# Nine instead of seven weight tiles ahead of two layer norms, with the first pair copied out of PSUM

## The chip, the core and the metric

The kernel runs on one core of a Trainium2 chip. The metric is device time per execution in microseconds (us). Before the change it is 1212.32 us, the median of three runs (1210.94 to 1214.39). The profile is of one execution of its own, which took 1212.16 us; its instructions span 1210.3 us of that, so 1.9 us lie around the span.

## The reference, cut to what matters

The reference computes two transformer blocks over 256 tokens of width 1024, in fp32. Block 2 has two layers. Each ends in a gated feed-forward network (FFN) that is fed by a layer norm:

```python
for l in range(DEPTH_2):                       # 2 layers
    y = even_mixer(...) if l % 2 == 0 else odd_mixer(...)
    x = layer_norm(alpha * x + y, ln_g[l, 0], ln_b[l, 0])       # the norm of this case
    y = conv_ffn(x, ffn_w_up[l], ffn_conv_w[l], ffn_conv_b[l], ffn_w_down[l])
    x = layer_norm(alpha * x + y, ln_g[l, 1], ln_b[l, 1])

def layer_norm(x, g, b):
    return (x - mu) * rsqrt(var + eps) * g + b
def conv_ffn(x, w_up, conv_w, conv_b, w_down):
    a, g = split(x @ w_up, 2)                  # w_up: 1024 x 5632
    return (gelu(causal_dwconv3(g) + conv_b) * a) @ w_down
```

The change touches the place where the layer norm `ln_g[l, 0]` runs into `x @ w_up`, in both layers.

## The kernel before

**Layout.** Activations lie feature by feature: 8 slices of 128 features on the partitions, 256 tokens along the row. `w_up` comes in 44 tiles of 1024 x 128 (512 KB each). One tile gives 128 output features, a *slice* here. Two slices (a and g of the same features) make a pair, and the gate needs both.

**Split arithmetic.** TensorE multiplies a rounded fp32 type, so each operand x is split into a high part h and a low part l = x - h. `wload` (L313) does it for weights: SP issues the DMA into `raw`, ScalarE casts `raw` to `hi` (L321), VectorE subtracts to `lo` (L322). A slice then takes 24 matmuls: 8 feature slices k, and for each hi times h (L329), hi times l (L330), lo times h (L331).

**The bridge.** A layer norm needs sums over all features of its input z, then a reciprocal square root on GpSimd, then a pass over z. TensorE would stand still meanwhile. So `layer_norm` (L1058) does two things side by side. It makes the normalized activations `nh`, `nl` in the usual way (L1076, L1077, and the split in L516 and L517). And through `raw_scaled` (L527) it makes `xh`, `xl` = z times g at once, with g and b as two more columns, so that the first weight tiles can be multiplied by these *raw* activations without waiting for the norm. Such a raw slice has 258 columns; when the row of means and deviations (`lnrow`, L1067) is there, `fix` (L1086) turns it into the right one: VectorE copies the two extra columns to `wgb` (L1090), ScalarE makes the shift from them (L1091), VectorE multiplies the slice in PSUM by the deviation row (L1093, out `sq`) and adds the shift (L1094, out `fx`). `NRAW` = 7 slices go this way: three pairs and the first slice of the fourth. From slice 8 on, `gemm_pairs` (L349) uses `nh` and `nl`.

**Banks.** PSUM has eight banks: four belong to the tag `a`, three to `g`, one to `m`. The raw slices take a whole bank each: the four `a`, then the three `g` (`places`, L1080). After them slice 8, whose partner is raw slice 7, takes the next `a` bank, and the later pairs go round four `a` and three `g` banks (`ring`, L623), a pair per bank. A bank can be written again when its last reader is done. For a raw slice that is VectorE's L1093.

**Order.** The order on each engine is worked out before the run by a scheduler that estimates times; each engine then runs its own list in that order, and waits at semaphores. `tc.high_priority` moves weight loads and the norm forward in it. The five buffers of `hi` and of `lo` are used in turn.

The bridge of layer 0 comes at 660 to 704 us of the span (bridge 1 here), that of layer 1 at 1005 to 1044 us (bridge 2). The norm in front of the odd mixer uses the same `layer_norm` with the tag `csb0` and its own number of raw slices.

Of the kernel before, what the change touches and what calls it, by code (L numbers as in the profile page):

```python
# [20 lines left out]
P = 128  # L21
S = 256
# [7 lines left out]
LAM_INIT = 0.8 - 0.6 * math.exp(-0.3 * 0)  # L30
MAGIC = 12582912.0
WPRI = 300
NRAW = 7
NRMS = 12
ORDER = ("kv0 ks w0 q w1 c0 tm c1 ckv kr CS0 CS1 CO0 kn CS2 CO1 CS3 CO2 kd CO3 cq uk uv uq DS0 DS1 DO0 DS2 DO1 DS3 "
         "DO2 DO3").split()
# [221 lines left out]
def _program(ctx, tc, nc, a, offs, dump):  # L258
    V, ACT, G, PE = nc.vector, nc.scalar, nc.gpsimd, nc.tensor
# [11 lines left out]
    pg = pool(ctx, "pg", 3, space=PSUM)  # L271
    pa = pool(ctx, "pa", 4, space=PSUM)
# [3 lines left out]
    def T(pl, shape, tag, dt=F32, **k):  # L276
        cnt[0] += 1
        return pl.tile(list(shape), dt, tag=tag, name="%s_%d" % (tag, cnt[0]), **k)
# [217 lines left out]
    def row_bcast(cols, at=None):  # L496
        rb = T(*(at or (pm,)), [P, len(cols) * P], "g" if at else "m")
        for j, c in enumerate(cols):
            mm(rb[:, j * P:(j + 1) * P], bc(c, [P, P]), ident, start=True, stop=True)
        return rb  # L500
# [13 lines left out]
    def split(src, h, l, scale=None):  # L514
        if scale is None:
            ACT.copy(h, src)  # L516
            tt(l, src, h, op=sub)  # L517
        else:
            act(h, src, AF.Copy, scale=scale)
            stt(l, src, scale, h, op0=mult, op1=sub)  # L520
# [6 lines left out]
    def raw_scaled(x, g, b, n):  # L527
        uh, ul = T(hp, [P, 8, n], "xh", F32R), T(hp, [P, 8, n], "xl", F32R)
        with tc.high_priority(LPRI):
            for c, v in zip(range(S, n), (g, b)):  # L530
                split(v, uh[:, :, c], ul[:, :, c])
            for k in range(8):
                act(uh[:, k, 0:S], x[:, k, :], AF.Copy, scale=g[:, k:k + 1])
                stt(ul[:, k, 0:S], x[:, k, :], g[:, k:k + 1], uh[:, k, 0:S], op0=mult, op1=sub)
        return dict(h=uh, l=ul, n=n)
# [505 lines left out]
    def ln_stats(z):  # L1041
        with tc.high_priority(LPRI):
            st = T(pm, [P, 4], "m")
            col_sums(st, [folded(*tiles(z, 8)), folded(*squares(z, 8))])
        return st

    def ln_rstd(st):
        nmu, mq = T(sm, [P, 2], "lnmu"), T(sm, [P, 2], "lnmq")
        act(nmu, st[:, 0:2], AF.Copy, scale=-1.0 / D)
        act(mq, st[:, 2:4], AF.Copy, scale=1.0 / D, bias=1e-5)  # L1050
        var = T(sm, [P, 2], "lnv")
        G.tensor_tensor(var, nmu, nmu, op=mult)
        G.tensor_tensor(var, mq, var, op=sub)
        r = T(sm, [P, 2], "lnr")
        G.tensor_tensor(r, var, mhalf[:, :2], op=ALU.pow)
        return nmu, r

    def layer_norm(z, g, b, h, l, xn, pl, tr_="lnrow", tf="fx"):  # L1058
        st = ln_stats(z)
        raw = raw_scaled(z, g, b, S + 2)  # L1060
        with tc.high_priority(LPRI):
            nmu, r = ln_rstd(st)
            nr = T(sm, [P, 2], "lnn")
            G.tensor_tensor(nr, nmu, r, op=mult)
            rb = row_bcast([r[:, 0:1], r[:, 1:2], nr[:, 0:1], nr[:, 1:2]])
            rs = T(pl, [P, 2, S], tr_)
            ACT.copy(rs.rearrange("p a s -> p (a s)"), rb)  # L1067
            rr, rn = rs[:, 0], rs[:, 1]
            for k, w in ((0, 1), (1, 1), (2, 2), (4, 2), (6, 2)):
                s2 = slice(k, k + w)  # L1070
                f = T(tp, [P, w, S], "sqa", bufs=2)
                u = T(tp, [P, w, S], "sq", bufs=3)
                for n in range(w):
                    c = k + n
                    act(f[:, n, :], rn, AF.Identity, scale=g[:, c:c + 1], bias=b[:, c:c + 1])  # L1075
                    stt(u[:, n, :], z[:, c, :], g[:, c:c + 1], rr, op0=mult, op1=mult)  # L1076
                tt(xn[:, s2, :], u, f, op=add)  # L1077
                split(xn[:, s2, :], h[:, s2, :], l[:, s2, :])

        places = iter([(pa, "a")] * 4 + [(pg, "g")] * 3)  # L1080

        def banks(n):
            raw["tiles"] -= n
            return [T(pl_, [P, raw["n"]], tag) for pl_, tag in (next(places) for _ in range(n))]

        def fix(rps):  # L1086
            f = T(pl, [P, 2, S], tf, bufs=2)
            for n in range(len(rps)):
                wgb = T(sm, [P, 2], "wgb")
                V.tensor_copy(wgb, rps[n][:, S:S + 2])  # L1090
                act(f[:, n, :], rn, AF.Identity, scale=wgb[:, 0:1], bias=wgb[:, 1:2])  # L1091
                t = T(tp, [P, S], "sq", bufs=3)
                tt(t, rps[n][:, 0:S], rr, op=mult)  # L1093
                tt(f[:, n, :], f[:, n, :], t, op=add)  # L1094
            return f

        raw.update(fix=fix, banks=banks, tiles=NRAW if tf == "fx" else NROD)
        return raw

# [709 lines left out]
    for i in range(2):  # L1809
        def norm(j, zt, xn):  # L1810
            g, b = C["ln_g%d%d" % (i, j)], C["ln_b%d%d" % (i, j)]
            return lambda h, l, pl, *tags: layer_norm(zt, g, b, h, l, xn, pl, *tags)

        if i == 1:
            with ExitStack() as ph:
                ap_ = pool(ph, "od", 1)
                cod = T(ap_, [P, a["cod"].shape[1]], "cod")
                nc.scalar.dma_start(cod, a["cod"])
                KO = {k: cod[:, o:o + n] for k, (o, n) in off_o.items()}
                W = T(ap_, [P, 8, S], "W")  # L1820
                nc.scalar.dma_start(W, hankel(0, 8))
                h, l = T(ap_, [P, 8, S], "oh", F32R), T(ap_, [P, 8, S], "ol", F32R)
                raw = norm_od(h, l, ap_, "ockv", "csb0")
                yh, yl = odd(ap_, h, l, W, KO, raw)
                z = T(xp, [P, 8, S], "x")
                gemm_pairs("od_out", range(4), 8, yh, yl, join=True, **residual_a(xa, z))
        dump("z%d0" % i, z)
        xa, z0 = T(xp, [P, 8, S], "x"), z
        z = T(xp, [P, 8, S], "x")
        ffn(norm(0, z0, xa), "g_up%d" % i, "g_dn%d" % i, C["gcw%d" % i], C["gcb%d" % i], False,  # L1830
            residual_a(xa, z))
        dump("z%d1" % i, z)
        if i == 0:
            xa = T(xp, [P, 8, S], "x")
            norm_od = norm(1, z, xa)
# [13 lines left out]
```

## Time and profile before

| | |
|---|---|
| median of three runs | 1212.32 us |
| profiled execution, and its span | 1212.16 us, 1210.3 us |
| TensorE busy | 1169.8 us, 97% |
| VectorE busy | 888.8 us, 73% |
| ScalarE busy | 691.8 us, 57% |
| GpSimd busy | 59.8 us, 5% |
| mean granted TensorE clock | 0.988 of full speed |

Busy time is the time in which an engine has an instruction in work. [...] The rows below give starts in us from the start of the span. [...]

### The profile page before, as it was taken

What the parts mean: (1) busy time and instruction counts of PE and PEld (TensorE: products, weight loads), DVE (VectorE), ACT (ScalarE), POOL (GpSimd) and SP (SyncE); (2) the same over time, 40 slices, a digit from 0 to 9 for tenths busy, and PEclk for the clock granted to TensorE, in tenths of its full rate; (3) what the DMA queues carried; (4) which work ended last, traced back from release to release, by engine and by line L of the source; (5) the groups of instructions that cost most, each with busy time, mean ns of one, the idle gap of its engine ahead of it and who ended that gap; (6) DMA issues with size and microseconds to landing.
All of it is one profiled execution on the core that took longest, in us unless ns stands there. A gap on an engine that the chain in (4) does not pass through costs nothing.

```text
span 1210.3 us, 23541 instructions
## 1 busy us (share of the span) xinstructions
PE 1169.8 (97%) x9370; PEld 1111.2 (92%) x9370; DVE 888.8 (73%) x1704; ACT 691.8 (57%) x1229; POOL 59.8 (5%) x61
## 2 busy tenths in 40 slices
PE   7889999999999999999999899999999999999997
PEld 7889989999999999899988899998988789999986
DVE  8969856866688887667565886667696768976654
ACT  5684544655566765446355675544675666755541
POOL 4000000100000000000001000001000001000010
PEclk9899999999999999999999999999998999999998
DMA  7424435664356556656423566656862125665560
GB/s 269 154 87 128 152 123 181 210 192 149 108 172 199 185 177 182 194 175 219 164 89 112 158 189 178 184 177 192 296 206 95 56 74 189 206 186 181 161 204 35
DMA packets 61276, 199.41 MB, mean 165 GB/s; under 512 B 8502, under 2 KB 12398, under 8 KB 60910
## 3 DMA queue, kind: packets, MB, share of 16 engines
q1 hardware_dynamic: 54864, 191.60, 49.7%
q10 hardware_dynamic: 6302, 6.32, 1.6%
q8 instruction: 73, 1.20, 0.4%
q14 instruction: 37, 0.30, 0.1%
HBM read 196.28 MB, written 1.60 MB: 163 GB/s over the span
## 4 chain that ended last, share of the span: by engine, by line
PE 85%; DVE 6%; ACT 3%; DMA 3%; issue 2%; POOL 1%; SPq 0%; DVEq 0%; ACTq 0%
PE g L330 11%; PE g L331 11%; PE g L329 11%; PE a L329 7%; PE a L330 7%; PE a L331 7%; PE a L394 5%; PE g L394 4%; PE a L396 3%; DVE lo L322 2%; PE g L340 2%; PE g L338 2%; PE g L339 2%; PE g L396 2%; DMA W<-vec 2%
## 5 line engine op out<-in xcount | busy, mean ns | idle before, releaser
L322 DVE TENSOR_TENSOR lo<-raw,hi 128x1024 fp32r<-128x1024 f32 (+3 forms) x359 | 427.9, 1196 | 185.8 <-ACT hi L321 178.1
L321 ACT CAST hi<-raw 128x1024 fp32r<-128x1024 f32 (+3 forms) x359 | 363.5, 1020 | 349.4 <-PE g L330 129.1
L329 PE MATMUL g<-xh,hi 128*128 128x256 f32 (+1 forms) x616 | 175.9, 286 | 8.1 <-ACT xh L569 7.9
L330 PE MATMUL g<-xl,hi 128*128 128x256 f32 (+1 forms) x624 | 179.4, 288 | 0.2
L331 PE MATMUL g<-xh,lo 128*128 128x256 f32 (+1 forms) x616 | 175.5, 285 | 1.3 <-DVE lo L322 1.2
L329 PE MATMUL a<-nh,hi 128*128 128x256 f32 x560 | 159.6, 286 | 4.6 <-ACT sqa L1075 2.8
L330 PE MATMUL a<-nl,hi 128*128 128x256 f32 x560 | 159.2, 285 | 0.9 <-DVE nl L517 0.9
L331 PE MATMUL a<-nh,lo 128*128 128x256 f32 x560 | 159.0, 284 | 0.0
L329 PEld LDWEIGHTS g<-xh,hi 128*128 128x128 f32 x616 | 117.4, 191 | 9.6 <-ACT xh L569 8.1
L330 PEld LDWEIGHTS g<-xl,hi 128*128 128x128 f32 x624 | 119.3, 191 | 1.5 <-DVE xl L570 0.7
L331 PEld LDWEIGHTS g<-xh,lo 128*128 128x128 f32 x616 | 117.0, 190 | 2.3 <-DVE lo L322 1.9
L329 PEld LDWEIGHTS a<-nh,hi 128*128 128x128 f32 x560 | 108.2, 194 | 5.7 <-ACT sqa L1075 2.9
L330 PEld LDWEIGHTS a<-nl,hi 128*128 128x128 f32 x560 | 108.3, 193 | 1.1 <-DVE nl L517 1.1
L331 PEld LDWEIGHTS a<-nh,lo 128*128 128x128 f32 x560 | 108.3, 193 | 0.0
L394 PE MATMUL a<-mx,hi 128*128 128x512 f32 x264 | 91.9, 394 | 0.0
L330 PE MATMUL g<-nl,hi 128*128 128x256 f32 x288 | 81.6, 283 | 0.0
L331 PE MATMUL g<-nh,lo 128*128 128x256 f32 x288 | 81.6, 283 | 0.0
L329 PE MATMUL g<-nh,hi 128*128 128x256 f32 x288 | 81.6, 283 | 0.0
L396 PE MATMUL a<-mx,lo 128*128 128x256 f32 x264 | 73.2, 278 | 0.0
L394 PE MATMUL g<-mx,hi 128*128 128x512 f32 x198 | 69.0, 395 | 0.0
L394 PEld LDWEIGHTS a<-mx,hi 128*128 128x128 f32 x264 | 49.5, 188 | 11.5
L331 PEld LDWEIGHTS g<-nh,lo 128*128 128x128 f32 x288 | 55.4, 192 | 0.0
(619 smaller groups left out, 2860.2 us busy)
## 6 DMA issues: line engine op xcount, KB each, us to landing
raw<-g_up SPq DMA_DIRECT2D x88, 512.0 KB, 3.6
raw<-f_up SPq DMA_DIRECT2D x44, 512.0 KB, 3.5
raw<-g_dn SPq DMA_DIRECT2D x32, 512.0 KB, 3.6
raw<-w_fm SPq DMA_DIRECT2D x27, 512.0 KB, 3.5
raw<-ev_fm SPq DMA_DIRECT2D x20, 512.0 KB, 3.8
raw<-f_dn SPq DMA_DIRECT2D x16, 512.0 KB, 3.6
raw<-od_fm SPq DMA_DIRECT2D x14, 512.0 KB, 4.2
raw<-g_dn SPq DMA_DIRECT2D x16, 384.0 KB, 3.4
```

Of the source, the lines that this page charges most:

```text
L321: ACT.copy(hi, raw)
L322: tt(lo, raw, hi, op=sub)
L329: mm(ps, hi[:, o:o + P], xh[:, k, :], start=start and k == 0, stop=False, skip_group_check=skip)
L330: mm(ps, hi[:, o:o + P], xl[:, k, :], start=False, stop=False, skip_group_check=skip)
L331: mm(ps, lo[:, o:o + P], xh[:, k, :], start=False, stop=stop and k == kt - 1, skip_group_check=skip)
L338: mm(ps, xh[:, k, t], hi[:, wsl], start=start and j == 0, stop=False, skip_group_check=skip)
L339: mm(ps, xh[:, k, t], lo[:, wsl], start=False, stop=False, skip_group_check=skip)
L340: mm(ps, xl[:, k, t], hi[:, wsl], start=False, stop=stop and j == len(ks) - 1, skip_group_check=skip)
L394: mm(f2, hi[:, o], X[:, k].rearrange("p a s -> p (a s)"), start=first and j == 0, stop=False, skip_group_check=True)
L396: mm(ps[:, 0, :], lo[:, o], X[:, k, 0, :], start=False, stop=last and j == len(ks) - 1, skip_group_check=True)
```

## The change

`NRAW` becomes 9, so raw slices 8 and 9 are added in the two bridges of block 2. The seven banks are full by then. So `fix`, when it is called for the first pair, first lets ScalarE copy both raw slices from PSUM into an SBUF tile `park`, and the rest of `fix` reads `park`. The two banks that this sets free, the first two `a` banks, are given to raw slices 8 and 9. The pairs are now four raw ones, and slice 9 with slice 10 as a mixed pair. The norm in front of the odd mixer is not changed.

```diff
-NRAW = 7
+NRAW = 9
@@ in layer_norm
-        places = iter([(pa, "a")] * 4 + [(pg, "g")] * 3)
+        parked = [2] if tf == "fx" else []
+        places = iter([(pa, "a")] * 4 + [(pg, "g")] * 3 + [(pa, "a")] * sum(parked))
...
         def fix(rps):
+            if parked:
+                parked.pop()
+                pk = T(pl, [P, 2, S + 2], "park")
+                for n in range(2):
+                    ACT.copy(pk[:, n, :], rps[n])
+                rps = [pk[:, n, :] for n in range(2)]
             f = T(pl, [P, 2, S], tf, bufs=2)
             for n in range(len(rps)):
                 wgb = T(sm, [P, 2], "wgb")
```

How the lists of the engines change, at three places of bridge 1 (bridge 2 is alike, with other buffer numbers). A number behind a name is that of the buffer; lines behind L1080 stand seven further down after the change, so that L1093 is L1100, and L1094 is L1101.

ScalarE, around the sums of the norm (`lnmu`), before:

```order
L321 CAST hi_8291<-raw_8289 128x1024 [waits DMAHW2_49,PE_49,Activation_49]
L1049 ACTIVATE lnmu_8029<-m_7978 128x2 [waits PE_49]
L1050 ACTIVATE lnmq_8030<-m_7978 128x2
L321 CAST hi_8344<-raw_8342 128x1024 [waits DMAHW3_49,PE_49,Activation_49]
L321 CAST hi_8374<-raw_8372 128x1024 [waits DMAHW4_49,PE_49,Activation_49]
L321 CAST hi_8422<-raw_8420 128x1024 [waits DMAHW5_49,DVE_49,PE_49]
L1067 COPY lnrow_8045<-m_8040 128x512 [waits PE_49]
```

And the same place with the change:

```order
L321 CAST hi_8294<-raw_8292 128x1024 [waits DMAHW2_49,PE_49,Activation_49]
L1092 COPY park_8151<-a_8089 128x258 [waits PE_49]
L1049 ACTIVATE lnmu_8029<-m_7978 128x2 [waits PE_49]
L1050 ACTIVATE lnmq_8030<-m_7978 128x2
L321 CAST hi_8348<-raw_8346 128x1024 [waits DMAHW3_49,PE_49,Activation_49]
L1092 COPY park_8151<-a_8090 128x258 [waits PE_49]
L321 CAST hi_8378<-raw_8376 128x1024 [waits DMAHW4_49,PE_49,Activation_49]
L321 CAST hi_8431<-raw_8429 128x1024 [waits DMAHW5_49,DVE_49,PE_49]
L1067 COPY lnrow_8045<-m_8040 128x512 [waits PE_49]
```

The two copies stand between the casts of weights, one of them ahead of `lnmu`; the casts keep their order.

TensorE, at the end of the twelfth slice of the FFN, before (`a_8489` is the pair of slices 11 and 12, `a_8559` the next pair):

```order
L329 MATMUL a_8489<-nh_7976,hi_8522 128x256
L330 MATMUL a_8489<-nl_7977,hi_8522 128x256
L331 MATMUL a_8489<-nh_7976,lo_8523 128x256
L329 MATMUL a_8559<-nh_7976,hi_8562 128x256 [waits Activation_49]
L330 MATMUL a_8559<-nl_7977,hi_8562 128x256
```

And with the change (`a_8506` is the pair of slices 11 and 12, `a_8576` the next one):

```order
L329 MATMUL a_8506<-nh_7976,hi_8539 128x256
L330 MATMUL a_8506<-nl_7977,hi_8539 128x256
L331 MATMUL a_8506<-nh_7976,lo_8540 128x256
L329 MATMUL a_8576<-nh_7976,hi_8579 128x256 [waits DVE_49,PE_49]
L330 MATMUL a_8576<-nl_7977,hi_8579 128x256
```

The same number of the FFN's matmuls lies behind this place in both lists. Before, the next pair waits for ScalarE, for its weights; now it waits for VectorE and TensorE, for its bank, which is that of raw slice 8 (`a_8345`).

VectorE, where that bank is read, with the change:

```order
L620 TENSOR_TENSOR ge_8171<-ge_8171,fx_8154 128x256 [waits Activation_49]
L606 SCALAR_TENSOR_TENSOR cv_8251<-fx_8238,consts_91,cv_8251 128x254 [waits DVE_49]
L322 TENSOR_TENSOR lo_8650<-raw_8647,hi_8649 128x1024 [waits DMAHW3_49,PE_49,Activation_49]
L322 TENSOR_TENSOR lo_8680<-raw_8677,hi_8679 128x1024 [waits DMAHW4_49,PE_49,Activation_49]
L517 TENSOR_TENSOR mx_8088<-ge_8171,mx_8088 128x256 [waits Activation_49]
L1101 TENSOR_TENSOR fx_8322<-fx_8322,sq_8326 128x256 [waits Activation_49]
L1097 COPY wgb_8491<-a_8428 128x2
L1101 TENSOR_TENSOR fx_8322<-fx_8322,sq_8332 128x256 [waits Activation_49]
L620 TENSOR_TENSOR ge_8255<-ge_8255,fx_8238 128x256 [waits Activation_49]
L1100 TENSOR_TENSOR sq_8416<-a_8345,lnrow_8045 128x256 [waits DVE_49]
L322 TENSOR_TENSOR lo_8720<-raw_8717,hi_8719 128x1024 [waits DMAHW5_49,PE_49,Activation_49]
L1100 TENSOR_TENSOR sq_8494<-a_8428,lnrow_8045 128x256 [waits DVE_49]
```

And before, where the first three banks are read that slices 8 to 12 take (raw slices 1, 2 and 3: `a_8089`, `a_8090`, `a_8173`):

```order
L1093 TENSOR_TENSOR sq_8155<-a_8089,lnrow_8045 128x256 [waits DVE_49]
L1077 TENSOR_TENSOR x_7971<-sq_8071,sqa_8070 128x512 [waits Activation_49]
L1094 TENSOR_TENSOR fx_8151<-fx_8151,sq_8155 128x256 [waits DVE_49]
L322 TENSOR_TENSOR lo_8523<-raw_8520,hi_8522 128x1024 [waits DMAHW0_49,Activation_49]
L517 TENSOR_TENSOR xl_10261<-consts_91,xh_10260 128x8 [waits Activation_49] x2
L1093 TENSOR_TENSOR sq_8161<-a_8090,lnrow_8045 128x256 [waits DVE_49]
L1093 TENSOR_TENSOR sq_8239<-a_8173,lnrow_8045 128x256 [waits DVE_49]
```

The reads of raw slices 8 (`sq_8416`) and 9 (`sq_8494`) stand behind the gelu products of the first two pairs and the subtractions of further weight tiles; the reads of raw slices 1 to 3 stood ahead of all that. Between the bridges the scheduler also moves some instructions of the odd mixer's attention on TensorE, VectorE and ScalarE; SP issues the same loads in the same order, and GpSimd's list is the same.

## Rows read from the trace of the kernel before

**Rows 1.** The page, part 1: busy us, share, instructions.

```profile
PE 1169.8 (97%) x9370; PEld 1111.2 (92%) x9370; DVE 888.8 (73%) x1704; ACT 691.8 (57%) x1229; POOL 59.8 (5%) x61
```

**Rows 2.** Waits of TensorE, whole span: releaser, us in total, times, longest.

```profile
PE a L329 <- ACT sqa L1075: 2.8, 1, 2.8
...
PE a L329 <- DVE sq L1093: 1.2, 1, 1.2
...
PE a L330 <- DVE nl L517: 0.9, 1, 0.9
...
PE a L329 <- DVE wgb L1090: 0.5, 1, 0.5
```

**Rows 3.** Timeline of TensorE, bridge 1: start us, us, instruction, [idle before].

```profile
683.10 0.28 PE L331 MATMUL g<-xh,lo 128*128 128x258 f32 x1
686.13 0.36 PE L329 MATMUL a<-nh,hi 128*128 128x256 f32 x1 [2.75 <-ACT sqa L1075]
...
687.13 0.38 PE L329 MATMUL a<-nh,hi 128*128 128x256 f32 x1
688.74 0.55 PE L329 MATMUL a<-nh,hi 128*128 128x256 f32 x1 [1.23 <-DVE sq L1093]
...
692.07 0.28 PE L331 MATMUL a<-nh,lo 128*128 128x256 f32 x1
...
693.38 0.28 PE L330 MATMUL a<-nl,hi 128*128 128x256 f32 x1
```

**Rows 4.** Stretches: us, PE, PEld, DVE, ACT, POOL busy, PEclk, DMA share, GB/s.

```profile
690.00:692.00 2.00, 2.00 (x11) 2.00 (x11) 2.00 (x6) 1.22 (x2) 0.00 (x0) 0.50 0.50 195
...
907.00:908.00 1.00, 0.51 (x2) 0.54 (x3) 1.00 (x9) 0.83 (x5) 0.00 (x0) 0.54 1.01 332
```

**Rows 5.** Timeline of VectorE, bridge 1.

```profile
678.02 1.67 DVE L1076 SCALAR_TENSOR_TENSOR sq<-x,consts,lnrow 128x256 f32<-128x256 f32 x4 [0.29 <-ACT lnrow L1067]
679.61 1.22 DVE L322 TENSOR_TENSOR lo<-raw,hi 128x1024 fp32r<-128x1024 f32 x1
...
685.61 0.42 DVE L1093 TENSOR_TENSOR sq<-a,lnrow 128x256 f32<-128x256 f32 x1
685.94 0.68 DVE L1077 TENSOR_TENSOR x<-sq,sqa 128x512 f32<-128x512 f32 x1
686.54 0.42 DVE L1094 TENSOR_TENSOR fx<-fx,sq 128x256 f32<-128x256 f32 x1
686.88 1.22 DVE L322 TENSOR_TENSOR lo<-raw,hi 128x1024 fp32r<-128x1024 f32 x1
...
688.18 0.74 DVE L1093 TENSOR_TENSOR sq<-a,lnrow 128x256 f32<-128x256 f32 x2
...
692.92 0.47 DVE L605 SCALAR_TENSOR_TENSOR cv<-fx,consts,cv 128x255 f32<-128x255 f32 x1
693.31 0.41 DVE L1094 TENSOR_TENSOR fx<-fx,sq 128x256 f32<-128x256 f32 x1
...
696.12 0.43 DVE L620 TENSOR_TENSOR ge<-ge,fx 128x256 f32<-128x256 f32 x1 [1.25 <-ACT ge L619]
```

**Rows 6.** Timeline of TensorE, bridge 2.

```profile
1027.17 0.28 PE L331 MATMUL g<-xh,lo 128*128 128x258 f32 x1
...
1031.31 0.39 PE L330 MATMUL a<-nl,hi 128*128 128x256 f32 x1 [0.92 <-DVE nl L517]
1031.53 0.28 PE L331 MATMUL a<-nh,lo 128*128 128x256 f32 x1
```

**Rows 7.** Timeline of VectorE, bridge 2.

```profile
1020.25 1.67 DVE L1076 SCALAR_TENSOR_TENSOR sq<-x,consts,lnrow 128x256 f32<-128x256 f32 x4
```

**Rows 8.** Timeline of ScalarE, bridges 1 and 2.

```profile
677.40 0.59 ACT L1067 COPY lnrow<-m 128x512 f32<-128x512 f32 x1 [1.37 <-PE m L499]
...
1019.10 0.59 ACT L1067 COPY lnrow<-m 128x512 f32<-128x512 f32 x1 [0.16 <-PE m L499]
```

**Rows 9.** ScalarE's copies of a row from PSUM: ns min/median/max.

```profile
L574 ACT COPY rs<-m x4: 365/372/373, 21.8 to 531.2; 128x256 f32<-128x256 f32 x4
```

## The prediction

> **What bounds the kernel now.** First the page: TensorE has an instruction in work for 97% of the span [rows 1], so a change counts only by what it does to the other 40 us or to TensorE's clock. Then the waits of TensorE over the whole span: four of them, 2.8, 1.2, 0.9 and 0.5 us, are at the two bridges [rows 2]. Then the timelines there. In bridge 1 the raw slices end with the matmul that starts at 683.10; the first matmul on `nh` starts at 686.13, after 2.75 us idle, the eighth at 688.74, after 1.23 us more [rows 3]. [...]
>
> The timeline of VectorE says what TensorE waits for there. The read of raw slice 1 starts at 685.61 and takes 0.42, so ends at 686.03, and TensorE starts 0.10 later; of the two reads from 688.18 the first ends at 688.60, and TensorE starts 0.14 later [rows 3, 5]. Those reads free the banks of slice 8 and of the pair behind it. So the banks, and not `nh`, end both waits of bridge 1, though the profile names ScalarE for the first. VectorE itself is without a pause there: each start follows the last by the cost of one instruction [rows 5].
>
> What bridge 1 loses before: the matmul at 692.07 is the 23rd on `nh` (seven until 687.13, fifteen from 688.74, then this one). At 0.12 each from 683.10 + 0.12 = 683.22 on it would have started at 683.22 + 22 x 0.12 = 685.86. **Loss 6.2 us**: 4.0 idle, 2.2 mostly from the half clock. In bridge 2 the last raw matmul starts at 1027.17 and the 16th on `nh` at 1031.53; undisturbed it would be 1027.29 + 15 x 0.12 = 1029.09. **Loss 2.4 us**, at full clock [rows 6].
>
> I compare both kernels at one point, E: the end of the FFN's twelfth slice, five slices or 120 matmuls behind raw slice 7. Undisturbed, E is at 683.22 + 14.4 = 697.6 and at 1027.29 + 14.4 = 1041.7. Before, with the losses, it is at 703.8 and 1044.1.
>
> **The change part by part.** *Raw slices 8 and 9.* They take 48 matmuls in place of 48 on `nh`, with 258 columns for 256, which is 48 x 0.12 x 2/258 = 0.04 us a bridge. They put the first matmul on `nh` off by 5.8 us, to 689.0 and 1033.1. That alone would cover both losses: 8.6 us, if nothing else came late.
>
> *Two copies on ScalarE a bridge.* No row has a copy of 258 columns from PSUM; the nearest take 0.37 us for 256 columns [rows 9] and 0.59 for 512 [rows 8]. I take 0.37; both cost nothing in bridge 1, where ScalarE is idle for 1.37 us ahead of `lnrow` and the copies fit in. In bridge 2 that gap is 0.16 [rows 8], while the casts ahead of it have some slack, so the norm starts 0 to 0.6 us later; I take 0.15.
>
> *VectorE.* A raw slice costs it a copy of few columns to `wgb` (0.08, below), a product (0.34) and a sum (0.34), so 1.5 us a bridge. The distances in its list are: subtraction of a weight tile 1.13 (its 1.22, less the 0.09 by which an instruction starts ahead of the end of the last, as at 685.94), an instruction of few columns 0.08 (two of them stand between that subtraction and the reads: 688.18 - 686.88 - 1.13 = 0.17), 512 columns 0.60 (685.94 to 686.54), 256 columns 0.34 (686.54 to 686.88), convolution step 0.39 (692.92 to 693.31), and 0.40 for one of the four of L1076 (678.02 to 679.61) [rows 5]. It waits for nothing new; what counts is what stands in its list ahead of the reads that free banks.
>
> *The new wait.* The pair of slices 11 and 12 takes the bank of raw slice 4, the next pair that of raw slice 8. Its read (`sq_8416`) stands far down VectorE's list, behind these, counted from the norm's first instruction at 678.02: eight of L1076 (3.2), seven weight subtractions (7.9), six of 512 columns (3.6), twenty of 256 (6.7), four convolution steps (1.6), and small ones (0.5), together 23.5 us. So the read cannot start before 701.5. Besides, the first gelu product waits for ScalarE's table load, which before left VectorE idle for 1.25 us [rows 5], and the weight tile behind it about 0.3: 703.1. With 0.42 for the read and 0.10 to TensorE, **E is passed at 703.6** in bridge 1 (bounds 702.0 and 703.6 from the idle time) against 703.8 before: **-0.2 us** (-1.8 to -0.2). TensorE is at E before that: the reads of raw slices 3 and 4 and the last `nl` let it lose some 2.6 us between 689 and 694, it gets to E at about 700.4, and waits 3.2.
>
> In bridge 2 the same sum starts at 1020.25 + 0.15 [rows 7]; one more weight subtraction and one 256-column instruction less stand ahead of the read: 24.1 us, so 1044.5; with 1.2 idle 1045.7, and **E is passed at 1046.2** (bounds 1045.0 and 1046.2) against 1044.1: **+2.1 us** (+0.9 to +2.1). TensorE arrives at 1041.9 with hardly a loss, and waits 4.3 us in one piece. There the raw slices before ended 8.1 us behind `lnrow`'s start, in bridge 1 only 5.7 [rows 3, 6, 8], so bridge 2 has little to win, while VectorE's list is as long in both.
>
> [...]
>
> *The clock after the new waits.* Before, 2.75 us idle were followed by seven matmuls at full clock, and only behind 1.23 us more did it fall; from 688.74 to 692.07 fifteen matmuls took 3.33 us for 1.80, so 1.5 us lost [rows 3, 4]. At 907 us it fell too, at a smaller wait [rows 4]; in bridge 2 it did not, at 0.9 and 0.5 [rows 2]. So each new wait costs 0 to 1.5 us. The wait of 4.3 us is nearest to the 4.0 of bridge 1 before: 1.5. That of 3.2 in one piece is nearest to 2.75, behind which seven matmuls ran at full clock: 0. [...]
>
> *The rest.* Weight loads keep their order, and a bank or weight that comes late behind E is nowhere in sight: the read of raw slice 9 is due 1.5 us behind that of slice 8 and wanted 5.8 us later. In the odd mixer the scheduler changes the order around a stretch with waits and half clock (907 us [rows 4]); I can't tell the sign and put 0, with 2 us to each side.
>
> *Sum.* -0.2 + 2.1 + 1.5 = +3.4 us on the profiled execution's 1212.16: **1215.5 us**. That execution lies 0.2 us below the median of the runs, which changes nothing.
>
> **The rivals.** *Fast: the extra slices cover the norm and the bank of slice 8 is free in time.* Then both losses go: 1212.2 - 8.6 = 1203.6, or about 1208 with half of it. For it: TensorE gets 5.8 us more work ahead of the norm, more than 4.0 idle. Against it: the read would have to be done by 697.6 and 1041.7, and VectorE's instructions ahead of it alone end at 701.5 and 1044.5. Chance 0.10.
>
> *Neutral: waits as summed, no fall of the clock.* 1212.2 + 1.9 = 1214.1; less, about 1212, if VectorE meets the lower bounds. For it: the clock held through bridge 2's waits. Chance 0.25.
>
> *Slower: the wait at raw slice 8's bank brings the half clock in both bridges.* 1.5 us more: 1217.0. It decides where TensorE's idle time, 3.2 us, is long enough; the rows have falls behind shorter waits (907 us). Chance 0.25.
>
> *My forecast,* one fall: 0.40, with its own range 1213.5 to 1217.5 from the odd mixer.
>
> **How the numbers follow.** Within 0.3% of 1212.32 means 1208.7 to 1216.0, about what a measurement of this kernel tells from no change. Faster: nearly all of the fast rival and a little of the neutral one through the odd mixer, 0.10. Slower: three quarters of the slower rival and four tenths of the forecast, 0.36. The same: 0.54. The range takes all but the ends: 1209.5, which leaves out most of the fast rival, to 1218.5.
>
> **What would show it.** Right: in the new profile the waits of 2.75 and 1.23 us are gone or shifted, and TensorE has a wait of 2 to 3.5 us near 700 to 704 and one of 3 to 4.5 near 1042 to 1046 ended by L1100 reading an `a` bank, with the clock at 0.5 behind the second; `lnrow` starts within 0.6 us of before. Wrong: no wait for L1100 in the thirteenth slice, or E at 698 and 1042; then the sum down VectorE's list is wrong. Or the twelve slices go as said, and the difference comes from the odd mixer.

## The result and the profile after

The changed kernel takes **1223.14 us** (median of six runs, 1221.77 to 1223.52) against 1211.86 us before (six runs): ratio 1.0085, 95% interval 1.0075 to 1.0096. Timed once more beside the kernel before, it took 1221.68 against 1212.30 us: 1.0081 (1.0064 to 1.0098). Forecast were 1215.5 us and a range up to 1218.5, with a chance of 0.54 for no change and 0.36 for slower: the sign of the sum was right, its size some 70% too small.

The profiled execution took 1222.87 us (span 1220.8, before 1210.3). Its largest waits of TensorE that are new or changed (releaser, us in total, times, longest):

```profile
PE a L329 <- DVE sq L1100: 6.7, 3, 4.1
PE g L329 <- DVE xh L1593: 3.2, 1, 3.2
PE a L330 <- DVE nl L517: 1.3, 2, 0.9
PE g L330 <- DVE ocx L570: 1.0, 1, 1.0
```

The waits of 2.8 and 1.2 us [rows 2] are gone. In their place stand three for reads of raw slices (L1100), two for `nl`, and two that the prediction did not have, for `xh` (L1593) and `ocx`: they lie in the odd mixer. TensorE in both bridges, where it waited:

```profile
691.86 0.39 PE L330 MATMUL a<-nl,hi 128*128 128x256 f32 x1 [0.42 <-DVE nl L517]
693.74 0.39 PE L330 MATMUL a<-nl,hi 128*128 128x256 f32 x1 [0.90 <-DVE nl L517]
695.46 0.39 PE L329 MATMUL a<-nh,hi 128*128 128x256 f32 x1 [0.75 <-DVE sq L1100]
...
705.31 0.36 PE L329 MATMUL a<-nh,hi 128*128 128x256 f32 x1 [1.77 <-DVE sq L1100]
...
1052.19 0.55 PE L329 MATMUL a<-nh,hi 128*128 128x256 f32 x1 [4.14 <-DVE sq L1100]
```

The last two are the first matmuls of slice 13 in either bridge. VectorE at the reads of raw slice 8 (704.74 and 1051.63), with the start of the norm in bridge 2:

```profile
704.74 0.42 DVE L1100 TENSOR_TENSOR sq<-a,lnrow 128x256 f32<-128x256 f32 x1
...
1026.40 1.67 DVE L1076 SCALAR_TENSOR_TENSOR sq<-x,consts,lnrow 128x256 f32<-128x256 f32 x4
...
1051.63 0.42 DVE L1100 TENSOR_TENSOR sq<-a,lnrow 128x256 f32<-128x256 f32 x1
```

The reads start 25.5 us behind the norm's first instruction in bridge 1 (679.26) and 25.2 in bridge 2; the prediction summed to 25.1 and 25.3. TensorE goes on 0.14 to 0.15 us behind the end of the read.

Where the clock was low (columns as in [rows 4]):

```profile
618.00:620.00 2.00, 2.00 (x11) 2.00 (x11) 0.91 (x5) 1.79 (x4) 0.00 (x0) 0.50 0.24 94
696.00:698.00 2.00, 2.00 (x11) 2.00 (x10) 2.00 (x7) 0.64 (x2) 0.00 (x0) 0.50 0.60 236
706.00:708.00 2.00, 2.00 (x12) 2.00 (x11) 2.00 (x7) 0.42 (x1) 0.00 (x0) 0.50 0.78 178
957.00:959.00 2.00, 2.00 (x11) 1.86 (x9) 1.92 (x9) 0.00 (x0) 0.00 (x0) 0.50 0.00 0
1053.00:1055.00 2.00, 2.00 (x11) 2.00 (x11) 2.00 (x7) 1.52 (x4) 0.00 (x0) 0.50 0.72 238
```

Two more lie at 912 and 929 us (0.50 in both); the kernel before had them too, at 907 and 928. So seven stretches at half clock behind 600 us, against three. (The one in which every profile ends, here 0.50 from 1215 us on, where TensorE has no work left, is left out here and below.)

**Where the time went.** Both kernels issue 9370 matmuls, and in most of the program in the same order, so the start of the n-th matmul can be set against the start of the n-th before. The difference grows in six places. The table gives the growth in us over the first profile of before, in three profiles of the changed kernel (the second and third are from E10 and E11 below):

| stretch (n-th matmul) | forecast | first | second | third |
|---|---|---|---|---|
| start, up to 613 us (4980) | 0 | -0.3 | +0.6 | -0.2 |
| 613 to 630 us (to 5110) | 0 | +1.6 | 0.0 | +3.0 |
| bridge 1 to slice 13 (5500 to 5662) | -0.2 | +0.2 | -0.2 | -0.2 |
| behind it (to 5800) | 0 | +1.6 | +0.1 | +0.1 |
| odd mixer, first half (6800 to 7480) | 0 (-2 to +2 for both halves) | -1.8 | -2.8 | -0.1 |
| odd mixer, second half (to 7610) | 0 | +4.9 | +3.5 | +3.6 |
| bridge 2 to slice 13 (8050 to 8196) | +2.1 | +2.1 | +2.1 | +2.1 |
| behind it (to 8300) | +1.5 | +2.4 | +1.6 | +1.5 |
| sum with small rests | +3.4 | +10.4 | +4.6 | +9.9 |

The two lines on slice 13 hold as forecast. The rest came from the second half of the odd mixer and from stretches at half clock.

The odd mixer first. TensorE there:

```profile
949.98 0.37 PE L329 MATMUL g<-ocx,hi 128*128 128x256 f32 x1
...
954.39 0.39 PE L329 MATMUL g<-ocx,hi 128*128 128x256 f32 x1 [3.19 <-DVE xh L1593]
955.80 0.58 PE L330 MATMUL g<-ocx,hi 128*128 128x256 f32 x1 [1.02 <-DVE ocx L570]
...
959.51 1.12 PE L1157 MATMUL m<-epT,ovs 128*64 128x256 f32 x4
```

VectorE there, with the change and, in the last two lines, before:

```profile
947.38 1.92 DVE L1525 TENSOR_SCALAR csb<-csb,cden 128x128 f32<-128x128 f32 x8
...
953.91 0.43 DVE L1593 TENSOR_TENSOR xh<-g,rs 64x256 f32<-64x256 f32 x1
```

```profile
943.70 1.92 DVE L1518 TENSOR_SCALAR csb<-csb,cden 128x128 f32<-128x128 f32 x8
...
951.93 0.43 DVE L1586 TENSOR_TENSOR xh<-g,rs 64x256 f32<-64x256 f32 x1
```

The second step of the product from `ocx` needs a `g` bank that VectorE has to read first (the wait ends with the fourth of eight products of L1592 and L1593, the one at 953.91), and the step behind it needs the low part of `ocx`. TensorE stands idle for 4.2 us, and the clock is at half speed behind. The last attention matmuls on `epT` (959.51) come after it. In the order of before they stand in between and fill that wait, as the lines under E8 show. VectorE's list has changed too: the eight scalings (947.38) now stand behind four instructions of the attention (L1149) that they stood ahead of before (943.70), and the fourth product ends 4.4 us behind the first step of the product from `ocx` (949.98) in place of 2.7 (949.68 before).

### The profile page after: what moved, and what is told of

The parts are those of the page before. It is cut to its first block, busy times and chain, and to the rows that moved or that the text cites. A ratio compares the mean times of both kernels' runs of the same rounds, so it can differ in the third digit from the quotient of the medians.

```text
span 1220.8 us, 23568 instructions
## 1 busy us (share of the span) xinstructions
PE 1175.2 (96%) x9370; PEld 1115.7 (91%) x9370; DVE 892.1 (73%) x1716; ACT 695.9 (57%) x1237; POOL 59.7 (5%) x61
## 4 chain that ended last, share of the span: by engine, by line
PE 85%; DVE 8%; ACT 3%; issue 2%; DMA 1%; POOL 0%; SPq 0%; DVEq 0%; ACTq 0%
PE g L330 12%; PE g L331 12%; PE g L329 11%; PE a L329 7%; PE a L330 7%; PE a L331 7%; PE a L394 5%; PE g L394 4%; PE a L396 3%; DVE lo L322 2%; PE g L340 2%; PE g L338 2%; PE g L339 2%; PE g L396 2%; PE a L961 1%
## 5 line engine op out<-in xcount | busy, mean ns | idle before, releaser
L329 PE MATMUL a<-nh,hi 128*128 128x256 f32 x528 | 152.1, 288 | 6.7 <-DVE sq L1100 6.7
L330 PE MATMUL a<-nl,hi 128*128 128x256 f32 x528 | 152.2, 288 | 1.3 <-DVE nl L517 1.3
L331 PE MATMUL a<-nh,lo 128*128 128x256 f32 x528 | 151.7, 287 | 0.0
L329 PEld LDWEIGHTS a<-nh,hi 128*128 128x128 f32 x528 | 103.8, 197 | 7.5 <-issue 7.4
L330 PEld LDWEIGHTS a<-nl,hi 128*128 128x128 f32 x528 | 103.8, 197 | 1.8 <-DVE nl L517 1.7
L331 PEld LDWEIGHTS a<-nh,lo 128*128 128x128 f32 x528 | 104.0, 197 | 0.0
L329 PEld LDWEIGHTS g<-nh,hi 128*128 128x128 f32 x288 | 55.3, 192 | 0.0
```

The lines of the kernel that those rows point to most:

```text
L329: mm(ps, hi[:, o:o + P], xh[:, k, :], start=start and k == 0, stop=False, skip_group_check=skip)
L330: mm(ps, hi[:, o:o + P], xl[:, k, :], start=False, stop=False, skip_group_check=skip)
L331: mm(ps, lo[:, o:o + P], xh[:, k, :], start=False, stop=stop and k == kt - 1, skip_group_check=skip)
```

## The experiments

For eight of them the table gives the growth in the same stretches, again in us over the first profile of before.

| | median us | bridge 1 to slice 13, behind | odd mixer, halves | bridge 2 to slice 13, behind | ratio (95%) |
|---|---|---|---|---|---|
| E1 bridge 1 only | 1216.02 | +0.2, +1.6 | -1.6, +4.9 | 0.0, 0.0 | 1.0026 (1.0015 to 1.0038) |
| E2 bridge 2 only | 1216.65 | -0.1, 0.0 | -2.5, +0.1 | +2.1, +1.5 | 1.0032 (1.0020 to 1.0045) |
| E3 ring turned | 1206.44 | -1.7, 0.0 | -1.7, +0.1 | -2.3, 0.0 | 0.9938 (0.9918 to 0.9958) |
| E4 park alone | 1211.44 | -2.0, 0.0 | -1.2, +0.1 | +1.7, 0.0 | 0.9996 (0.9982 to 1.0010) |
| E5 ten raw | 1205.51 | -5.9, 0.0 | -1.4, +3.4 | -2.5, 0.0 | 0.9947 (0.9929 to 0.9965) |
| E7 ScalarE frees 8, 9 | 1206.39 | -6.1, 0.0 | -1.1, +3.6 | -2.5, 0.0 | 0.9958 (0.9941 to 0.9975) |
| E8 mixer restored | 1203.01 | -5.7, 0.0 | -1.5, 0.0 | -2.5, 0.0 | 0.9931 (0.9918 to 0.9944) |
| E9 7 and 8 freed | 1204.68 | -5.7, +1.3 | -1.5, 0.0 | -2.5, +1.5 | 0.9949 (0.9933 to 0.9966) |

The kernel before took 1211.70 us beside E1 to E4, 1211.55 beside E5 to E7, 1211.12 beside E8 to E10. The first half of the odd mixer is 1.1 to 2.8 us shorter in nearly all, E12 (the kernel before itself) included: that much of it was half clock in the first profile of before.

**E1, one bridge changed.** The wide form is used for the first call of the norm only (the edits here and below are shortened):

```diff
-        parked = [2] if tf == "fx" else []
+        wide = tf == "fx" and WIDE.pop(0)      # WIDE = [True, False]
+        parked = [2] if wide else []
...
-tiles=NRAW if tf == "fx" else NROD
+tiles=NRAW if wide else 7 if tf == "fx" else NROD
```

> Nine raw slices and the parked pair in bridge 1 alone; bridge 2 as before. The order of the odd mixer is then that of the changed kernel. If the losses are those of places (bridge 1 +1.8 us, odd mixer +2.9), the time is 1211.9 + 4.7 = 1216.6 us, and 1218.1 if TensorE's clock also falls at 616 us as it did in the profile of the changed kernel (+1.5). Rival: the odd mixer's 2.9 us come from bridge 2's change or from chance, then 1213.7.

**E2, the other bridge.** `WIDE = [False, True]`.

> Nine raw slices and the parked pair in bridge 2 alone; the odd mixer has the order of the kernel before. If the losses are those of places, only bridge 2's 4.4 us remain: 1216.3 us (1217.8 with a fall of the clock at 616 us), with the odd mixer as before and a wait of about 4.1 us for the read of raw slice 8. Rival: the parts help each other, then under 1214 or above 1219.

1216.02 and 1216.65 us: both as the sum of places says (1216.6, 1216.3). Bridge 2 alone costs its wait of 4.14 us and the half clock behind (+1.5 us). Bridge 1 alone costs 0.2 us up to slice 13 and 1.6 of half clock behind it, but brings the order of the odd mixer with it, and with that +4.9 us. The excesses over before, 4.3 and 5.0 us, add up to 9.3, about the 9.4 to 11.3 of the whole change. E2's profile is of its fastest run (1213.41 us), and its places add up to 3.6 us; where the median loses 1.4 more no profile shows.

**E3, the banks in another order.**

```diff
-            ring = itertools.cycle([(pa, "a")] * RA + [(pg, "g")] * RG) if RA else None
+            k = 1 if raw["tiles"] == NRAW else RA
+            ring = itertools.cycle([(pa, "a")] * k + [(pg, "g")] * RG + [(pa, "a")] * (RA - k)) if RA else None
```

> The whole change, but the banks of the pairs behind raw slice 9 are taken in the order a, g, g, g, a, a, a in place of a, a, a, a, g, g, g, so that the pair of slices 13 and 14 takes the bank of raw slice 5 and the banks of raw slices 8 and 9 come three pairs later. If the read of raw slice 8 is what costs, the waits of 1.8 and 4.1 us there and the half clock behind them (1.5 and 2.3) go: bridge 1 ends 1.5 us earlier than in the kernel before, bridge 2 1.9 earlier; the odd mixer's order is nearly that of before: 1211.9 - 3.4 = 1208.5 us (1210 with the fall at 616 us). Rival: the banks of raw slices 5 to 7 come no earlier, or the wait moves on to the next pair, then 1220 or more.

1206.44 us, so faster than both, and by 2 us more than expected. In bridge 2 VectorE reads raw slice 5 (`sq<-g`) at 1031.97, where slice 13 is wanted at 1038.95; no wait is left in bridge 2, and the clock stays up (a stretch in which slice 13 runs):

```profile
1031.97 0.41 DVE L1100 TENSOR_TENSOR sq<-g,lnrow 128x256 f32<-128x256 f32 x1
```

```profile
1038.00:1042.00 4.00, 4.00 (x36) 4.00 (x35) 3.64 (x10) 4.00 (x7) 0.00 (x0) 1.00 0.16 36
```

Bridge 1 keeps the waits of 0.5, 0.9 and 0.75 us that lie ahead of slice 13. So the two raw slices were not the fault; it was which bank the next pair took. This is shown with the same copies, the same nine raw slices, and the mixer's order of before.

**E4, the copies without the slices.** `NRAW = 7` again, `places` as before, the copies kept.

> Seven raw slices as before, but the first pair is copied by ScalarE, so its banks go to slice 8 and the pair behind it. If the waits of the kernel before (2.75 and 1.23 us in bridge 1) are for banks, they go, and what is left is the wait for nh and nl: a loss of 2 to 3.5 us in place of 6.2 in bridge 1, 1 to 2 in place of 2.4 in bridge 2, so 1206.5 to 1209.5 us. Rival: the first of those waits is for nh (as the profile names it) and the copies put the norm off: 1211 to 1213.

1211.44 us: a miss, no change. The first pair's banks came free early: the first matmul on `nh` follows the raw slices without a wait, so the 2.75 us of before were for a bank and not for `nh`. Bridge 1 gained 2.0 us, and 3.2 us of idle time are left there, 1.11 for `nl`, 0.65 for `nh` and 1.45 for the read of a further raw slice:

```profile
681.70 0.50 PE L329 MATMUL a<-nh,hi 128*128 128x256 f32 x2
683.31 0.38 PE L330 MATMUL a<-nl,hi 128*128 128x256 f32 x1 [1.11 <-DVE nl L517]
...
687.58 0.35 PE L329 MATMUL a<-nh,hi 128*128 128x256 f32 x1 [1.45 <-DVE sq L1100]
```

In bridge 2 TensorE then waited for `nl` (one line of TensorE, two of VectorE):

```profile
1026.92 0.39 PE L330 MATMUL a<-nl,hi 128*128 128x256 f32 x1 [2.08 <-DVE nl L517]
```

```profile
1025.05 1.22 DVE L322 TENSOR_TENSOR lo<-raw,hi 128x1024 fp32r<-128x1024 f32 x1
1026.18 0.68 DVE L517 TENSOR_TENSOR nl<-x,nh 128x512 fp32r<-128x512 f32 x1
```

A weight subtraction stands ahead of `nl`, and a stretch at half clock follows (from 1027.5; a matmul's 0.28 us become 0.39 there). The copies alone move most of the waiting from the banks to `nl` and `nh`; the two belong together, the raw slices for the time and the copies for the banks.

**E5, ten raw slices** (E3 with):

```diff
-NRAW = 9
+NRAW = 10
-        parked = [2] if tf == "fx" else []
+        parked = [2, 2] if tf == "fx" else []     # each pair has a park tile of its own
```

> The kernel with the turned ring, and with ten raw slices in place of nine: ScalarE copies the first two pairs, and raw slices 8, 9 and 10 take three of their four banks. In bridge 1 the first matmul on nh comes 2.9 us later, so if the waits left there (0.5 and 0.9 us for nl, 0.75 for the bank of raw slice 4, and the half clock behind them, 1.5) come from nh and nl being late, they go: 1206.4 - 3.5 = 1203 us. Rival: the third raw pair and two more copies put the norm and VectorE's reads off by as much, or bridge 2 gets a new wait: 1206 to 1210.

1205.51 us. The waits of both bridges went, as expected (-5.9 and -2.5). But the odd mixer had the order of the changed kernel again, with its waits, which the expectation had not looked at:

```profile
945.45 0.39 PE L329 MATMUL g<-ocx,hi 128*128 128x256 f32 x1 [3.20 <-DVE xh L1593]
946.85 0.40 PE L330 MATMUL g<-ocx,hi 128*128 128x256 f32 x1 [1.02 <-DVE ocx L570]
```

**E6, the wait filled with work.** In slice 12, ahead of its last matmul:

```diff
+            for q in range(fill if k == kt - 1 else 0):      # 14 in bridge 1, 33 in bridge 2
+                mm(ps, C["zero"], xh[:, k, :], start=False, stop=False)
             mm(ps, lo[:, o:o + P], xh[:, k, :], start=False, stop=stop and k == kt - 1)
```

> The changed kernel, with matmuls by a tile of zeros ahead of the last matmul of slice 12: 14 in bridge 1 and 33 in bridge 2, 1.7 and 4.0 us, about as long as the waits of 1.8 and 4.1 us for the read of raw slice 8. They add nothing to the sums. The odd mixer has the order of before. If the half clock behind those waits comes from TensorE standing idle, it stays away, while the read comes no earlier: bridge 1 +0.3 and bridge 2 +2.1 against before, 1211.9 + 2.4 = 1214.3 us. Rival: the fall belongs to something else at that place and comes all the same: 1.5 and 2.4 more, 1218.2 us.

1216.55 us (ratio 1.0040, 1.0026 to 1.0054), between the two. Bridge 2 tells more: from matmul 8050 to 8300 of the changed kernel it takes 34.3 us with the 33 matmuls by zeros among them, where three profiles of the changed kernel took 36.1 to 36.9 and the kernel before took 32.4. The clock stayed up behind:

```profile
1044.00:1048.00 4.00, 4.00 (x36) 4.00 (x34) 4.00 (x9) 3.29 (x7) 0.00 (x0) 1.00 0.38 118
```

In all four profiles with that wait unfilled (three of the changed kernel, E2) it fell there. This points to TensorE's idle time as the cause of the half clock in bridge 2. It is one profile against four, though, and of the fastest of E6's twelve runs (1212.32 us at a mean granted clock of 0.991; the others have 0.985 to 0.990), so where the others lost their time is not shown. Bridge 1 says nothing: the tile of zeros changed VectorE's order there, and TensorE stood 4.76 us ahead of the first matmul on `nh`; the profile names no releaser.

```profile
692.62 0.55 PE L329 MATMUL a<-nh,hi 128*128 128x256 f32 x1 [4.76 <-issue]
```

**E7, the same ring, the banks freed by ScalarE.** The pairs that are copied become `parked = [2, 0, 0, 2, 1]` (the first pair, raw slices 7 and 8, and 9; five copies a bridge), taken from the front.

> The changed kernel, but ScalarE also copies raw slices 7, 8 and 9 from PSUM to SBUF, so the banks of 8 and 9 are free without VectorE's read; the order of the banks and the order of the odd mixer are those of the changed kernel. If the wait is for VectorE's place in its list, the waits of 1.8 and 4.1 us and the half clock behind them go as with the turned ring, and the odd mixer still costs its 2.9 us: 1223.1 - 9.8 = 1213.3 us, up to 1215 if the six copies put nh off. Rival: the wait stays, since ScalarE's copies come late in its own list: 1219 or more.

1206.39 us, better than expected by 7. No wait above 0.1 us is left in either bridge, those for `nl` included, so the whole 6.1 and 2.5 us come back; the odd mixer costs 3.6 where 2.9 were foretold. (There are five copies a bridge, not the six of the expectation.) With the ring of the changed kernel, it was VectorE's place in its list, and not the bank's as such, that cost.

**E8, the odd mixer.** `parked = [2, 0, 2, 2, 1]`.

> As the kernel in which ScalarE frees the banks of raw slices 8 and 9, and with the pair of raw slices 5 and 6 copied too; by this the planner gives the odd mixer nearly the order of before (15 matmuls of 400 stand elsewhere there, not 143). If that order is what costs 3.6 us there, the same bridges now give 1206.4 - 3.6 = 1202.8 us. Rival: the wait for the uk product's reads in the odd mixer does not hang on the order, then 1206 again, or two more copies put nh off, 1205 or more.

1203.01 us, as expected. TensorE at the product from `ocx`:

```profile
942.39 0.38 PE L329 MATMUL g<-ocx,hi 128*128 128x256 f32 x1 [0.38 <-ACT ocx L569]
...
943.93 0.65 PE L1157 MATMUL m<-epT,ovs 128*64 128x256 f32 x2 [0.40 <-ACT epT L1541]
...
946.24 0.38 PE L329 MATMUL g<-ocx,hi 128*128 128x256 f32 x1
947.02 0.43 PE L1157 MATMUL m<-epT,ovs 128*64 128x256 f32 x1 [0.40 <-ACT epT L1541]
...
947.81 0.38 PE L329 MATMUL g<-ocx,hi 128*128 128x256 f32 x1
```

The attention matmuls lie between the first and the third matmul of that product, and the wait of 4.2 us is 1.4 in four pieces. E7 and E8 have the same bridges to 0.5 us and differ by 3.6 us there. In the bridges:

```profile
688.00:700.00 12.00, 12.00 (x97) 11.64 (x97) 11.10 (x25) 8.41 (x16) 0.00 (x0) 1.00 0.45 132
1022.00:1036.00 14.00, 14.00 (x119) 14.00 (x118) 12.69 (x26) 10.36 (x18) 0.00 (x0) 1.00 0.68 226
```

TensorE is busy without a break at full clock. This version beats both kernels, by 8.1 us against before (0.9931, 0.9918 to 0.9944).

**E9, without raw slice 9's copy.** `parked = [2, 0, 0, 2, 0]`.

> The changed kernel, but ScalarE also copies raw slices 7 and 8, and not 9; the odd mixer has nearly the order of before (8 matmuls stand elsewhere). The wait at the bank of raw slice 8 goes; that of raw slice 9 is read by VectorE some 1.5 us behind the place where 8 was read and wanted 5.8 us later, so it should cost nothing in bridge 1 and at most 0.5 us in bridge 2: 1203 to 1203.5 us. Rival: the wait moves to the bank of raw slice 9 and takes the clock down: 1206 or more.

1204.68 us, 1.2 to 1.7 more than expected. The wait moved one pair on, to the bank of raw slice 9, since TensorE now arrives 6 us earlier; the clock held (matmuls 0.12 us apart behind both waits). In bridge 1 the profile names ScalarE, but VectorE's read of raw slice 9 ends at 704.46, 0.15 us ahead of the matmul:

```profile
704.61 0.36 PE L329 MATMUL a<-nh,hi 128*128 128x256 f32 x1 [1.10 <-ACT fx L1098]
...
1042.49 0.36 PE L329 MATMUL a<-nh,hi 128*128 128x256 f32 x1 [1.29 <-DVE sq L1100]
```

**E10, the changed kernel again.** No edit.

> The changed kernel once more, for a second profile. If the fall of the clock at 616 us is chance (up to there the order is that of before, and no other profile has it), it may be away now; the half clock behind the waits at 705 and 1052 us and in the odd mixer at 955 us should be there again, and the steps between fixed matmuls be the same within 0.3 us but for the falls. Rival: the fall at 616 us belongs to the changed kernel and is there again.

One run, 1217.01 us. The waits are as in the first profile, or longer where no half clock had delayed TensorE (2.85 us at slice 13 of bridge 1). But the clock is up at four of the seven places, 618, 696 and 706 us among them:

```profile
618.00:620.00 2.00, 2.00 (x17) 1.74 (x16) 1.65 (x9) 1.34 (x3) 0.00 (x0) 1.00 0.49 183
695.00:697.00 2.00, 2.00 (x19) 2.00 (x19) 2.00 (x6) 0.38 (x1) 0.00 (x0) 1.00 0.81 254
705.00:707.00 2.00, 2.00 (x19) 2.00 (x18) 2.00 (x7) 0.36 (x2) 0.00 (x0) 1.00 0.58 168
953.00:955.00 2.00, 2.00 (x11) 2.00 (x11) 1.92 (x9) 0.00 (x0) 0.00 (x0) 0.50 0.00 0
1048.00:1050.00 2.00, 2.00 (x11) 2.00 (x11) 2.00 (x7) 1.52 (x4) 0.00 (x0) 0.50 0.62 248
```

**E11, the changed kernel timed again.** No edit.

> The changed kernel once more, now timed beside the kernel before, since its two profiles differ by 5.9 us, all of it in stretches at half clock: 1222.9 with seven of them behind 600 us, 1217.0 with three. If the number of falls changes from run to run, its times spread from 1215 to 1223.5 with a median of about 1219 us, and the ratio to before is about 1.006. Rival: 1217.0 was the exception, then 1222 to 1223.5 again.

1221.68 us (1219.40 to 1223.50): higher than expected, so 1217.0 was at the low end. Its profile has five stretches at half clock, again one near 617 us (0.50 from 617 to 621). E10 and E11 ran on different chips (beside them the kernel before took 1211.12 and 1212.30 us), so what is chance and what is the chip is not told apart.

**E12, the kernel before again.** Seven blank lines in the source.

> The kernel before with seven blank lines in its source, for a second profile. The waits of 2.75 and 1.23 us in bridge 1 and of 0.5 and 0.9 us in bridge 2 should be the same within 0.1 us, since they come from the order; the stretches at half clock (689, 907 and 928 us in the first profile) may differ in number and length, and the time with them, 1208 to 1215.5 us. Rival: they are the same three, then 1211.5 to 1212.5.

One run, 1213.25 us. The waits are those of [rows 3] within 0.2 us, the stretches at half clock again three (in the first, a matmul takes 0.41 us in place of 0.28), near the same places but of other lengths:

```profile
687.59 0.35 PE L329 MATMUL a<-nh,hi 128*128 128x256 f32 x1 [2.77 <-ACT sqa L1075]
...
690.21 0.55 PE L329 MATMUL a<-nh,hi 128*128 128x256 f32 x1 [1.04 <-DVE sq L1100]
```

## Why the prediction was wrong

**The waits at raw slice 8's bank: right.** Forecast were -0.2 us at slice 13 of bridge 1 and +2.1 of bridge 2; three profiles give -0.2 to +0.2 and +2.1. The sum down VectorE's list was right to 0.4 us in 25, in bridge 2 partly by luck. There 24.1 us of work and 1.2 idle were put (its own terms, 23.5 + 1.13 - 0.34, give 24.3); measured are 24.5 and 0.75, since VectorE waited 0.23 us at the first gelu product and 0.52 behind it, not 1.2:

```profile
1047.34 0.42 DVE L620 TENSOR_TENSOR ge<-ge,fx 128x256 f32<-128x256 f32 x1 [0.23 <-ACT ge L619]
```

E3 and E7 show the cause from two sides, by taking the bank from another tile and by freeing it on another engine. In the first profile of the changed kernel the last matmul of raw slice 8 in bridge 1 starts at 687.19, and VectorE, which has work ahead of that read in its list, reads it at 704.74.

**The losses of before: right.** 6.2 and 2.4 us were worked out; E7 and E8 got 5.7 to 6.1 and 2.5 back. The 0.12 us a matmul behind them is what the changed kernel shows too: its raw slices 8 and 9 of bridge 1, 48 matmuls, start from 684.45 to 690.09, so 0.120 us apart. E4 confirms that the first wait was for a bank. The fast rival's 1203.6 us is what E8 measured (1203.0). Its condition, a bank that is free in time, did not hold in the kernel as changed.

**The half clock behind the waits: right in bridge 2, open in bridge 1.** 1.5 us were put in bridge 2 (1.5, 1.6 and 2.4 measured; E6 points to the idle time as the cause). In bridge 1 nothing was put: true in two profiles, where the clock held behind a wait of 2.85 us, and 1.6 in the first (and in E1), behind one of 1.77. There the clock had fallen once already, at 695 us in the first and at 694 in E1. The slower rival, a fall behind the waits of both bridges, came true in the first profile alone. A half clock came behind the 4.14 us in all three profiles, and behind the 2.85 us in neither of two; how long a wait has to be for it is not shown.

**The odd mixer: the step that failed.** "In the odd mixer the scheduler changes the order around a stretch with waits and half clock (907 us); I can't tell the sign and put 0, with 2 us to each side." It cost 3.5 to 4.9 us, and not at 907 but at 950 us. (The first half gained 0.1 to 2.8 us, but E12, with the order of before, gained 1.1 there too.) The attention matmuls that had stood between the first two steps of the product from `ocx` were moved behind it, so TensorE comes to the second step 2.6 us sooner after the first, and the bank comes free 1.7 us later after it, with VectorE's list changed as well. Idle 4.2 us in place of 1.4 is +2.8; the rest, 0.7 to 2.1, goes with the fall of the clock behind it. The other kernels bear it out: +3.4 to +4.9 in E1, E5 and E7, 0.0 to +0.1 in E2, E3, E4, E8 and E9. Both orders stood in the lists ahead of the run, as those around the bank of raw slice 8 did; that a sum down them would have given the cost is not shown.

**The half clock at 616 us: in no step.** It cost 1.6, 0 and 3.0 us in three profiles. Up to there all lists are those of the kernel before. None of the other 11 profiles has it. No idle time precedes it: in both profiles TensorE has an instruction in work throughout (here the first; columns as in [rows 4]; the fall begins at 617).

```profile
614.00:618.00 4.00, 4.00 (x23) 2.63 (x20) 4.00 (x14) 1.63 (x6) 0.00 (x0) 0.89 0.22 51
```

Chance, the chip, or something of this program that the lists don't show: that stays open, and with it up to 3 us of the 9.4 to 11.3.

With 3.5 for the odd mixer the forecast's own sum would have been +6.9, so 1219 us; most of what is left to 1223 lies in the clock. One slip changes nothing: the parts of the chance of slower add up to 0.35, not 0.36.

## What to carry to other kernels

Whoever lends a buffer to one more tile should follow it to its next user, and sum the reader's list up to the read that frees it; if that comes late, lend another buffer or let another engine free it. A change of order far from the edit is part of the change: price it with the same sum, list by list, and don't put it at zero with a margin. And compare two kernels by the starts of equal instructions, in more than one profile, since that parts what the order costs from what the clock adds.

## What was not expected of the hardware

- The same changed kernel took 1217.0 to 1223.5 us, and between its profiles of 1222.9 and 1217.0 the waits of the bridges agree to 0.1 us, but for the one that a half clock ahead of it shortened (1.77 against 2.85). The number of stretches at half clock went from seven to three, and the difference is theirs. The same three waits (0.4 to 0.5, 0.9 and 0.75 us) were followed by half clock near 695 us in the first profile (0.50), E1 and E3, and not in E10 (1.00) and E11. The three profiles of one kernel have seven, three and five such stretches.
- With 33 matmuls by a tile of zeros in place of 4.1 us of idle time the clock was at 1.00 behind them (E6, one profile).
- ScalarE's copy of 258 columns out of PSUM takes 0.37 us, as 256 columns did [rows 9]; the norm's row starts no later for it in either bridge (the norm's first instruction 0.0 and 0.2 us).
